# Row dot products and a softmax: the first load whole, a clearing ahead of the first y, all rows summed on VectorE, code that runs on

## The chip, the cores and the metric

The kernel runs on one core of a Trainium2 chip. The metric is the device time of one execution in microseconds (us). The kernel before takes 320.85 us, the median of three runs (320.79 to 320.87).

## The reference

The inputs x and y have the shape (8, 4096, 512) in float32. The reference forms the whole product of x and y transposed for each batch and keeps only its diagonal; what is computed is the dot product of each row of x with the same row of y, and a softmax over the 4096 dots of a batch.

```python
gram = np.matmul(x, y.transpose(0, 2, 1))
diag = np.diagonal(gram, axis1=1, axis2=2)
diag = diag - diag.max(axis=-1, keepdims=True)
exp = np.exp(diag)
return (exp / exp.sum(axis=-1, keepdims=True)).astype(np.float32)
```

## The kernel before

**Tiling.** A batch is spread over 32 partitions (G), so four batches (Q) fill the 128 partitions, and there are two groups of four. Each partition then holds 128 rows (C) of its batch. A step takes 32 rows (R) for each partition: 128 x 32 x 512 float32, which is 8.39 MB of x and as much of y. Four steps make a group, and there are eight steps (S), t = 0 to 7.

**Buffers.** There are two buffers for x (`xs`, step t uses number t % 2), one for y (`ys`) and a small one (`side`) for a copy of the last K = 6 rows of y. The dots go to `diag`, one column for each row, and `res` holds the softmax of a group.

**A step in the loop (t = 0 to 5, lines 118 to 131).** SP issues the load of x (`load_x`, line 63) and the load of y (`load_y`, line 66). ScalarE copies the last six rows of y to `side` (line 123). VectorE multiplies x by y in place: the first 26 rows from `ys`, then the last six from `side` (`products`, line 70). So `ys` can be loaded anew when the product of 26 rows and the copy are through. Then the products are summed along each row: VectorE takes the first 30 rows in one reduction (`sums`, line 73), and ScalarE the last two (W), row by row, with a copy that accumulates (`sums_act`, line 78). When both are through, the x buffer can be loaded for step t + 2.

**The first step** loads x in two parts: two rows (0.5 MB) and then thirty (7.86 MB). The y load and the x load of step 1 follow on SP without a wait.

**The order of work.** The schedule is written by hand: each engine runs its instructions in the order of the program. All loads are issued by SP and stand in one queue, in the order x(0), y(0), x(1), y(1) and so on. An issue waits for the buffer to be free, and everything behind it on SP waits with it.

**The end.** Step 6 (lines 133 to 139) loads y in two halves and multiplies each half as it lands; ScalarE sums its first 24 rows and VectorE the other eight. Step 7 (lines 141 to 150) is loaded in pieces of 16, 8, 4, 2, 1 and 1 rows, and VectorE forms the dot of each row in one instruction (`dots`, line 83). The softmax of the first group is computed between steps 3 and 4 (`exps`, `normalize`), that of the second at the end.

**Code alignment.** Lines 115 and 116 ask that the next instruction of VectorE and of ScalarE begin a block of 128 places of code. The code ahead of it then ends in a branch over the unused places.

Of the kernel before, what the change touches and what calls it, by code (L numbers as in the profile page):

```python
# [1 line left out]

# [5 lines left out]


@with_exitstack
def kernel(
    ctx: ExitStack,
    tc: tile.TileContext,
    x: bass.AP,
    y: bass.AP,
    out: bass.AP,
):
    nc = tc.nc
    ctx.enter_context(tc.manual_schedule())  # L20
    f32 = mybir.dt.float32
    Alu = mybir.AluOpType
    Act = mybir.ActivationFunctionType
    X = mybir.AxisListType.X
    B, N, D = x.shape
    P = nc.NUM_PARTITIONS
    G = 32
    Q = P // G
    C = N // G
    R = 32  # L30
    H = R // 2
    K = 6
    W = 2
    S = B // Q * (C // R)


    xv = x.rearrange("(s b) (j c) d -> s (b j) c d", b=Q, j=G)
    yv = y.rearrange("(s b) (j c) d -> s (b j) c d", b=Q, j=G)
    ov = out.rearrange("(s b) (j c) -> s (b j) c", b=Q, j=G)

    big = ctx.enter_context(tc.tile_pool(name="big", bufs=1))
    small = ctx.enter_context(tc.tile_pool(name="small", bufs=1))


    xs = [big.tile([P, R, D], f32, name=f"xs{i}") for i in range(2)]
    ys = big.tile([P, R, D], f32, name="ys")
    side = big.tile([P, K, D], f32, name="side")

    diag = [small.tile([P, C + i], f32, name=f"diag{i}") for i in range(B // Q)]
    res = [small.tile([P, C], f32, name=f"res{i}") for i in range(B // Q)]  # L50

    def columns(t, r0, n):
        c0 = t % (C // R) * R + r0
        return slice(c0, c0 + n)

    def rows(t, r0, n):
        return xs[t % 2][:, r0 : r0 + n, :]

    def dots_of(t, r0, n):
        return diag[t * R // C][:, columns(t, r0, n)]  # L60

    def load_x(t, r0, n):
        nc.sync.dma_start(out=rows(t, r0, n), in_=xv[t * R // C, :, columns(t, r0, n), :])  # L63

    def load_y(t, r0, n):
        nc.sync.dma_start(out=ys[:, r0 : r0 + n, :], in_=yv[t * R // C, :, columns(t, r0, n), :])  # L66

    def products(t, r0, n, yt):
        xt = rows(t, r0, n)
        nc.vector.tensor_tensor(out=xt, in0=xt, in1=yt, op=Alu.mult)  # L70

    def sums(t, r0, n):
        nc.vector.tensor_reduce(out=dots_of(t, r0, n), in_=rows(t, r0, n), axis=X, op=Alu.add)  # L73

    def sums_act(t, r0, n):
        for r in range(r0, r0 + n):
            row = xs[t % 2][:, r, :]
            nc.scalar.activation(out=row, in_=row, func=Act.Copy, accum_out=dots_of(t, r, 1))  # L78

    def dots(t, r0, n):  # L80
        for r in range(r0, r0 + n):
            xt = xs[t % 2][:, r, :]
            nc.vector.scalar_tensor_tensor(  # L83
                out=xt, in0=xt, scalar=1.0, in1=ys[:, r, :], op0=Alu.mult, op1=Alu.mult,
                accum_out=dots_of(t, r, 1),
            )

    def over_quadrant(name, column, op, negate=False):

        got = small.tile([P, 1], f32, name=name)  # L90
        nc.vector.tensor_reduce(  # L91
            out=got, in_=column.to_broadcast([P, G]), axis=X, op=op, negate=negate, apply_transpose=True
        )
        return got

    def largest(out, d):
        nc.vector.tensor_reduce(out=out, in_=d, axis=X, op=Alu.max)  # L97

    def exps(i, d):
        mxp = small.tile([P, 1], f32, name=f"mxp{i}")  # L100
        largest(mxp, d)
        nmx = over_quadrant(f"nmx{i}", mxp, Alu.max, negate=True)
        sump = small.tile([P, 1], f32, name=f"sump{i}")
        nc.scalar.activation(out=res[i], in_=diag[i][:, :C], func=Act.Exp, bias=nmx, scale=1.0, accum_out=sump)  # L104
        return sump

    def normalize(i, sump):
        total = over_quadrant(f"sum{i}", sump, Alu.add)
        rc = small.tile([P, 1], f32, name=f"rc{i}")
        nc.vector.reciprocal(out=rc, in_=total)  # L110
        nc.vector.tensor_single_scalar(out=res[i], in_=res[i], scalar=rc, op=Alu.mult)  # L111

    nc.vector.addr_align(128, offset=0, max_nops=0)
    nc.scalar.addr_align(128, offset=0, max_nops=0)

    for t in range(S - 2):
        if t == 0:
            load_x(t, 0, 2)  # L120
        load_x(t, 2 if t == 0 else 0, R - 2 if t == 0 else R)
        load_y(t, 0, R)
        nc.scalar.activation(out=side, in_=ys[:, R - K :, :], func=Act.Copy)  # L123
        if t == C // R:
            normalize(0, sump)
        products(t, 0, R - K, ys[:, : R - K, :])
        products(t, R - K, K, side)
        sums(t, 0, R - W)
        sums_act(t, R - W, W)
        if t == C // R - 1:  # L130
            sump = exps(0, diag[0])

    t = S - 2
    load_x(t, 0, R)
    for r0 in (0, H):
        load_y(t, r0, H)
        products(t, r0, H, ys[:, r0 : r0 + H, :])
    sums(t, R - H // 2, H // 2)
    sums_act(t, 0, R - H // 2)

    t += 1
    r0 = 0
    for n in (16, 8, 4, 2, 1, 1):
        if r0 < R - 1:
            load_x(t, r0, max(n, 2))
        load_y(t, r0, n)
        if r0 == R - 2:
            largest(diag[1][:, C:], diag[1][:, : C - 2])
        dots(t, r0, n)
        r0 += n  # L150

    met = small.tile([P, C - R], f32, name="met")
    nc.scalar.activation(out=met, in_=diag[1][:, : C - R], func=Act.Copy)  # L153

    for p, n in ((0, G), (G, G), (2 * G, G), (3 * G, G)):
        nc.sync.dma_start(out=ov[0, p : p + n, :], in_=res[0][p : p + n, :])
    normalize(1, exps(1, diag[1][:, C - 2 :]))
    nc.scalar.dma_start(out=ov[1], in_=res[1])


# [1 line left out]
_INS = ['x', 'y']  # L162
_OUTS = [((8, 4096), 'float32')]


# [23 lines left out]
```

## Time and profile before

| What | Value |
|---|---|
| median of three runs | 320.85 us (320.79 to 320.87) |
| span of the profiled execution | 318.9 us (318.87) |
| data moved | 134.37 MB, a mean of 421 GB/s |
| VectorE busy | 244.7 us, 77% of the span |
| ScalarE busy | 42.0 us, 13% |
| reduction of 30 rows (line 73) | 16.153 us each, six of them |
| reduction of 8 rows (line 73) | 4.420 us |
| product of 26 rows and of 6 rows (line 70) | 14.026 and 3.351 us |
| product of 16 rows, 128 x 8192 (line 70) | 8.684 us |
| ScalarE's sum of one row (line 78) | 0.616 us and 0.186 us to read it out |
| first issue of a load | 0.73 us after the span's start |
| first y lands | 42.33 us |

The profile shows one execution of 318.9 us; the medians of the runs hold about 2 us more than that span. Busy time is a sum over the span; which work sets the end is read from the chain of work that ended last, which is followed back from the last instruction, and from the share of time in which the 16 DMA engines carry packets. An issue on SP is the moment at which a load is handed to the queue, and a load lands when its last byte has been reported. A DMA packet here is one row of memory for one partition: up to 64 KB for a load of 32 rows.

### The profile page before, as it was taken

The page shows a single profiled execution, that of the slowest core. Times are in us where ns is not written, and L with a number is a line of the kernel's source. Part 1 is how long each engine was busy: PE and PEld are TensorE (multiplying, and loading weights), DVE is VectorE, ACT ScalarE, POOL GpSimd, SP SyncE. Part 2 cuts the span into 40 slices and gives each one's busy share as a digit, 9 for nine tenths or more (in the row PEclk, how much of TensorE's full clock was granted, in tenths as well). Part 3 has the DMA queues.
Part 4 walks back from the last instruction along what each step waited for, and adds up shares of the span by engine and source line. Part 5 has one row for each costly group of instructions (what it writes and reads, how often), then busy time and mean ns, then how long its engine had stood idle before and what let it go on. Part 6 is the DMA issues. An engine that isn't in the chain of part 4 may idle for free.

```text
span 318.9 us, 304 instructions
## 1 busy us (share of the span) xinstructions
DVE 244.7 (77%) x96; ACT 42.0 (13%) x84; POOL 0.2 (0%) x4
## 2 busy tenths in 40 slices
DVE  0000069995899939999399994999949999996995
ACT  1000030100301003010120103000030100197000
POOL 0000000000000000000000000000000000000000
DMA  8989999999999999999999999999999899999993
GB/s 314 493 378 485 436 395 436 485 395 403 510 403 395 477 444 395 427 493 395 403 510 403 395 460 460 395 419 493 403 395 510 358 444 415 444 423 419 421 413 116
DMA packets 4226, 134.37 MB, mean 421 GB/s; under 512 B 512, under 2 KB 768, under 8 KB 1536
## 3 DMA queue, kind: packets, MB, share of 16 engines
q1 hardware_dynamic: 4080, 134.29, 97.8%
q10 hardware_dynamic: 144, 0.07, 0.1%
q14 instruction: 2, 0.02, 0.0%
HBM read 134.22 MB, written 0.13 MB: 421 GB/s over the span
## 4 chain that ended last, share of the span: by engine, by line
DMA 62%; DVE 35%; issue 2%; SPq 0%; ACT 0%; DVEq 0%
DMA ys<-in_y_dram 62%; DVE xs L70 30%; DVE diag L73 4%; DVE xs L83 0%; SPq L63 0%; DVE res L111 0%; DVE nmx L91 0%; DVE sum L91 0%; ACT res L104 0%; DVE rc L110 0%; DVE mxp L97 0%; DVEq L70 0%; SPq L66 0%; DVEq L83 0%
## 5 line engine op out<-in xcount | busy, mean ns | idle before, releaser
L70 DVE TENSOR_TENSOR xs<-xs,ys 128x13312 f32<-128x13312 f32 (+1 forms) x8 | 101.4, 12690 | 66.5 <-DMA ys<-in_y_dram 66.5
L73 DVE TENSOR_REDUCE diag<-xs 128x30 f32<-128x15360 f32 (+1 forms) x7 | 101.3, 14477 | 0.2
L78 ACT ACTIVATE xs<-xs 128x512 f32<-128x512 f32 x36 | 22.2, 616 | 111.0 <-DVE xs L70 111.0
L123 ACT ACTIVATE side<-ys 128x3072 f32<-128x3072 f32 x6 | 16.6, 2764 | 124.0 <-DMA ys<-in_y_dram 124.0
L83 DVE SCALAR_TENSOR_TENSOR xs<-xs,ys 128x512 f32<-128x512 f32 x32 | 19.9, 686 | 3.3 <-DMA ys<-in_y_dram 3.3
L70 DVE TENSOR_TENSOR xs<-xs,side 128x3072 f32<-128x3072 f32 x6 | 20.1, 3351 | 0.0
L78 ACT ACTIVATION_READ_ACCUMULATOR xs<-xs 128x1 f32 x36 | 6.7, 186 | 0.0
L104 ACT ACTIVATE res<-diag,nmx 128x128 f32<-128x128 f32 x2 | 0.8, 402 | 37.6 <-DVE nmx L91 37.6
L83 DVE DVE_READ_ACCUMULATOR xs<-xs,ys 128x1 f32 x32 | 2.6, 81 | 0.0
L123 ACT ACT_TABLE_LOAD x1 | 1.3, 1283 | 1.2 <-PEq L173 1.2
L91 DVE TRANSPOSE_TENSOR_REDUCE sum<-sump 128x1 f32<-128x32 f32 x2 | 0.4, 212 | 1.2 <-ACT res L104 1.2
L111 DVE TENSOR_SCALAR res<-res,rc 128x128 f32<-128x128 f32 x2 | 0.6, 286 | 0.1
L97 DVE TENSOR_REDUCE mxp<-diag 128x1 f32<-128x128 f32 (+1 forms) x2 | 0.4, 220 | 0.1
L91 DVE TRANSPOSE_TENSOR_REDUCE nmx<-mxp 128x1 f32<-128x32 f32 x2 | 0.4, 212 | 0.1
L110 DVE RECIPROCAL rc<-sum 128x1 f32<-128x1 f32 x2 | 0.3, 164 | 0.1
L104 ACT ACTIVATION_READ_ACCUMULATOR res<-diag,nmx 128x1 f32 x2 | 0.4, 186 | 0.0
L97 DVE TENSOR_REDUCE diag<-diag 128x1 f32<-128x126 f32 x1 | 0.3, 284 | 0.1
L153 ACT ACTIVATE met<-diag 128x96 f32<-128x96 f32 x1 | 0.3, 282 | 0.0
L173 POOL MEMSET const-bfloat16-1.0<- 128x1 bf16 x1 | 0.1, 102 | 0.0
L173 POOL MEMSET const-uint8-127<- 128x1 uint8 x1 | 0.1, 102 | 0.0
L173 POOL MEMSET const-float32-0.0<- 128x1 f32 x1 | 0.1, 99 | 0.2 <-issue 0.2
L173 POOL MEMSET const-float32-1.0<- 128x1 f32 x1 | 0.1, 99 | 0.0
## 6 DMA issues: line engine op xcount, KB each, us to landing
ys<-in_y_dram SPq DMA_DIRECT2D x3, 4096.0 KB, 16.0
xs<-in_x_dram SPq DMA_DIRECT2D x1, 7680.0 KB, 21.8
xs<-in_x_dram SPq DMA_DIRECT2D x1, 4096.0 KB, 14.9
xs<-in_x_dram SPq DMA_DIRECT2D x1, 2048.0 KB, 20.5
ys<-in_y_dram SPq DMA_DIRECT2D x1, 2048.0 KB, 17.2
xs<-in_x_dram SPq DMA_DIRECT2D x3, 512.0 KB, 22.1
xs<-in_x_dram SPq DMA_DIRECT2D x1, 1024.0 KB, 19.3
ys<-in_y_dram SPq DMA_DIRECT2D x1, 1024.0 KB, 21.3
```

The costliest lines, as they stand in the source:

```text
L70: nc.vector.tensor_tensor(out=xt, in0=xt, in1=yt, op=Alu.mult)
L73: nc.vector.tensor_reduce(out=dots_of(t, r0, n), in_=rows(t, r0, n), axis=X, op=Alu.add)
L78: nc.scalar.activation(out=row, in_=row, func=Act.Copy, accum_out=dots_of(t, r, 1))
L83: nc.vector.scalar_tensor_tensor(out=xt, in0=xt, scalar=1.0, in1=ys[:, r, :], op0=Alu.mult, op1=Alu.mult, accum_out=dots_of(t, r, 1),)
L91: nc.vector.tensor_reduce(out=got, in_=column.to_broadcast([P, G]), axis=X, op=op, negate=negate, apply_transpose=True)
L97: nc.vector.tensor_reduce(out=out, in_=d, axis=X, op=Alu.max)
L104: nc.scalar.activation(out=res[i], in_=diag[i][:, :C], func=Act.Exp, bias=nmx, scale=1.0, accum_out=sump)
L110: nc.vector.reciprocal(out=rc, in_=total)
L111: nc.vector.tensor_single_scalar(out=res[i], in_=res[i], scalar=rc, op=Alu.mult)
L123: nc.scalar.activation(out=side, in_=ys[:, R - K :, :], func=Act.Copy)
L153: nc.scalar.activation(out=met, in_=diag[1][:, : C - R], func=Act.Copy)
L173: nc = _bacc.Bacc("TRN2", target_bir_lowering=False, num_devices=1)
```

## The change

The two alignment lines go. Step 0 loads its x like the other steps, in one load of 32 rows. Ahead of the y load of step 0, VectorE writes zeros to the first 16 rows of `ys`, and the load waits for that, since it writes the same rows. In steps 0 to 5 VectorE's reduction takes all 32 rows and ScalarE sums none; W is no longer needed. Step 6 keeps its sums on ScalarE.

```diff
     K = 6
-    W = 2
     S = B // Q * (C // R)
...
-    nc.vector.addr_align(128, offset=0, max_nops=0)
-    nc.scalar.addr_align(128, offset=0, max_nops=0)
-
     for t in range(S - 2):
+        load_x(t, 0, R)
         if t == 0:
-            load_x(t, 0, 2)
-        load_x(t, 2 if t == 0 else 0, R - 2 if t == 0 else R)
+            nc.vector.memset(ys[:, :H, :], 0.0)
         load_y(t, 0, R)
         nc.scalar.activation(out=side, in_=ys[:, R - K :, :], func=Act.Copy)
         if t == C // R:
             normalize(0, sump)
         products(t, 0, R - K, ys[:, : R - K, :])
         products(t, R - K, K, side)
-        sums(t, 0, R - W)
-        sums_act(t, R - W, W)
+        sums(t, 0, R)
         if t == C // R - 1:
             sump = exps(0, diag[0])
```

## The prediction

> **What bounds the kernel now.** I read the page's summary first, then the chain of work that ended last, then the DMA view in narrow windows.
>
> ```profile
> span 318.9 us, 304 instructions
> DVE 244.7 (77%) x96; ACT 42.0 (13%) x84; POOL 0.2 (0%) x4
> q1 hardware_dynamic: 4080, 134.29, 97.8%
> q14 instruction: 2, 0.02, 0.0%
> ```
>
> No engine is full, but the one data queue keeps all 16 DMA engines busy 97.8% of the span. The middle of the chain says the same:
>
> ```profile
> 1.65 40.68 DMA ys<-in_y_dram
> ...
> 81.12 14.04 DVE xs L70
> 95.16 0.02 SPq L66
> 95.18 0.03 issue
> 95.21 24.52 DMA ys<-in_y_dram
> 119.73 0.03 issue
> 119.75 0.02 DVEq L70
> 119.78 0.04 issue
> 119.82 14.04 DVE xs L70
> 133.86 0.02 SPq L66
> 133.88 0.03 issue
> 133.91 24.52 DMA ys<-in_y_dram
> ```
>
> The reader is to see where the y loads land: 42.33, 119.73 and 158.43 us. The last two are 38.70 apart, for 16.78 MB (one x and one y of 8.39 MB), which is 433.5 GB/s, or 27.1 per DMA engine. The chain seems to pass through VectorE's products, but during these 14 us the load of x that was queued earlier fills the DMA engines. So the end is the start of the first load, plus all bytes at 433.5 GB/s, plus a tail, as long as each load is issued before the one ahead of it has run out. The windows that follow show the two places where that can change; a digit is the busy share of one slot, a number under it the GB/s that began in the slot.
>
> The window 114 to 122 us, in slots of 0.2 us:
>
> ```profile
> DMA  9070000009999070000007999070000007999770
> GB/s 1638 0 328 0 0 0 0 0 0 655 983 1638 1638 0 328 0 0 0 0 0 0 328 983 1638 1966 0 328 0 0 0 0 0 0 328 983 1311 1966 328 328 0
> ```
>
> Each engine begins a packet of 64 KB every 2.4 us. The group from 118.2 to 119.4 is the first of the x load that was issued at 114.67, and it follows the group before without a gap. The window 3 to 5 us, in slots of 0.05 us:
>
> ```profile
> DMA  9939599999299938999909099000900000000000
> GB/s 410 328 164 573 246 246 246 328 328 246 82 1393 2540 1311 164 246 246 1393 1311 2458 0 4997 0 2458 1311 0 0 0 1229 0 0 0 0 0 0 0 0 0 0 0
> ```
>
> The high numbers are the 16 engines going over from the 4 KB packets of the two-row load to the 60 KB packets of the other thirty rows, the first at 3.55 us and the last at 4.40 to 4.45.
>
> **The change, part by part.**
>
> *x of step 0 in one load.* The two-row load is 8 packets of 4 KB on each engine. The first begins at 1.75 us (the window 0 to 2 us is empty before). At 27.1 GB/s an engine needs 8 x 0.151 = 1.21 us for them; the last engine is through only at 4.45, as if it had begun at full rate at 3.24. With one load, each engine goes straight into 64 KB packets. If all engines began at 1.75, the gain were 3.24 - 1.75 = 1.49 us. If their first packets were spread as widely as those long packets, 0.9 us, the gain were 0.59. The trace has no first packet of 64 KB, so these are the bounds, with a gain of nothing kept as a rival. I take the middle, **-1.0 us**. Nothing takes it back on the way: every later load stands in the same queue, and y lands when the DMA is through.
>
> *The clearing.* 128 x 8192 elements on VectorE. The nearest row is the product of that size, 8.68 us; from 0.8 us it ends at 9.5, and SP issues y of step 0 then instead of at 1.65. It is needed when the first engine is through with x, 1.75 + 19.35 = 21.1 us, less the 1.0 us from an issue (0.73) to its first packet (1.75): about 20.1. So 10.6 us are spare, and even at twice the row (17.4 us) it is hidden. Behind the waiting issue on SP stands only x of step 1, needed after y, near 41 us. VectorE has nothing to do before 42.46. Against a slower DMA beside VectorE: y of step 0 landed 19.35 us after x (22.98 to 42.33) with VectorE idle, and half of 38.70 is also 19.35. Cost 0; without the cover, 8.7.
>
> *The sums.* VectorE reduces 32 rows instead of 30 in six steps. The rows with 30 (16.153 us) and 8 (4.420 us) give 0.533 us a row, so 17.22, which is +1.07. SP's issue of x two steps on waits for this reduction (76.02, 114.67 and so on): 114.67 becomes 115.73. VectorE then works 14.03 + 3.35 + 17.22 = 34.6 us of each 38.7, so it stays ahead, and y, issued behind the products, isn't moved. The first engine asks for that x at 118.2, so the issue has 2.47 us in place of 3.53, against the 1.0 us of the first load. The later issue is hidden, **0**, by the last packet of y on each engine; without this cover it costs up to 1.07 on each of six loads. ScalarE loses 12 row sums that ended at 99.8 when VectorE's ended at 114.6; nobody waits for them: 0. The step after the loop begins its products 1.07 us later against the DMA, so the first y of the last step is issued at 279.1 instead of 278.04; the x ahead of it lands at 284.3 (269.44 + 14.9), so 5.2 us are left: 0. VectorE ends that step's reduction at 292.1, and the y lands at 294.04: 0. From there every row dot follows a landing and moves with it.
>
> Here a page speaks against the change. The Trainium skill's "DMA: Bandwidth & Descriptors" (Specifications; Latency and other measured facts) has 0.6 us to a first byte from SP, and up to 2 us for an HBM access at high load. An estimate from it is 2.6 us, 0.1 more than the issue has; six loads at 0.1 would make the sum 320.6. No row here shows a late issue under load.
>
> *No new code block.* The two branches at the start (0.72 on ScalarE, 0.76 on VectorE) go; nothing waited for them. The two instruction packets of 8 KB came at 1.75 to 3.5 us, after ScalarE had begun its table load at 1.16 behind the branch, so code is fetched ahead. Now the code runs on from the middle of a block, and the fetch of a next one may fall anywhere, or be left out. At 27.1 GB/s it takes one engine 0.30 us; both took 1.38 us of one engine's time at the start (4.3% of 16 engines for 2 us). A load lands with its slowest engine, so the cost lies between 0 and 1.38; the low end is the nearer, as one engine in sixteen is seldom the last. I take half a packet, **+0.15 us**.
>
> The page "Runtime: NRT & Kernel Launch" (Instruction fetch mechanics) calls the cost of passing into the next block mostly hidden, which would make the sum 319.85, and it has blocks of 16 KiB where the trace has packets of 8.
>
> The sum is -1.0 + 0.15 = -0.85 us on the profiled 318.87, so 318.02; the median of 320.85 lies 1.98 above that span, and I add the same: **320.0 us**.
>
> **The rivals.**
>
> - *The opening isn't shortened.* The delay to 4.45 us may come from the first accesses rather than from the packets' size, and long packets meet it too. For it: some engines take more than the others although each has 8 equal packets. Against it: a 64 KB packet holds 2.4 us of work to hide a late descriptor, a 4 KB one 0.15. Then 320.85 plus the code fetch, 320.7 to 321.1.
> - *The x loads come late*, the rival on the other side. Its place is the issue behind each of the six reductions; it decides once an issue under load takes more than 2.47 us to its first packet, and it costs six times the excess, at most 6 x 1.07 = 6.4. At 2.8 us it is +2.0, so 322.0; at the most 326.4. For it: the cover shrinks by a third. Against it: 1.0 us at the start, and no gap now.
> - *VectorE waits for code.* 66 of its 96 instructions run in the last 20 us, where it goes from dot to dot with about 0.6 us of gaps in all. A fetch that isn't ahead takes 1.0 us to its packet and half of the 1.38 for it, and behind a 64 KB packet 2.4 more: 1.7 to 4.1 us, less 0.6, so 321.1 to 323.5. Against it: the block behind the old branch was there already.
>
> **How the numbers follow.** The forecast gets 0.64, its own range being 319.3 (the whole 1.49 and no fetch) to 320.45 (0.59 and 0.2 of fetch); the opening without gain 0.14, late x loads 0.08, waiting for code 0.10, and something unseen 0.04, half to either side. Within 0.2% means within 0.64 us, about what a measurement of this kernel can tell from no change. Faster, under 320.21: 0.58 of the forecast and 0.02 unseen, 0.60. The same: 0.06 of the forecast, 0.12 of the first rival, 0.02 of the code, 0.20. Slower: 0.20. For 8 times in 10 the range takes the forecast and the first rival: 319.4 to 321.0.
>
> **What would show it.** Right: x of step 0 lands near 22.0 us, y of step 0 near 41.3, y loads still 38.70 apart, and x issues some 4 us ahead of a landing. If y loads stand further apart, the cover was too thin; if x lands near 23, the split cost nothing; if VectorE shows a gap of microseconds between dots, it waited for code. An instruction packet in the middle that shifts all later landings would mis-size my 0.15.

## The result

The changed kernel takes 321.31 us, the median of 12 runs (320.78 to 321.78), against 320.85 for the kernel before (12 runs, 320.65 to 320.99). The ratio is 1.0015, its interval 1.0008 to 1.0022: a little slower, by less than the 0.64 us that the prediction called a difference. The forecast of 320.0 was wrong, and 321.31 lies outside its range. Note the spread: 1.0 us now, 0.34 before; 9 of the 12 runs now lie above 321.0, none of the 12 before. The profiled execution belongs to a run of 320.97, so it is one of the better ones.

The summary of the page after the change:

```profile
span 319.2 us, 269 instructions
DVE 258.1 (81%) x97; ACT 33.9 (11%) x60; POOL 0.2 (0%) x4
q1 hardware_dynamic: 3936, 134.29, 97.7%
q14 instruction: 2, 0.02, 0.0%
```

VectorE has 13.4 us more work, ScalarE 8.1 less, and the data queue is as full as it was. So the bound is the same, and the difference has to be looked for where the queue starts, where it slips, and in the tail. The chain that ended last, after the change (start, duration, what):

```profile
2.50 6.90 DVE ys L117
9.40 0.02 issue
9.42 32.78 DMA ys<-in_y_dram
...
56.43 24.46 DMA ys<-in_y_dram
...
95.07 24.73 DMA ys<-in_y_dram
...
133.98 24.52 DMA ys<-in_y_dram
...
294.13 19.49 DMA ys<-in_y_dram
```

Three numbers tell the whole difference. The first y lands at 42.20 us (9.42 + 32.78), 0.13 earlier than before: that is all that the opening gained. The y of step 2 takes 24.73 us from issue to landing, where 24.52 is the rule: the x ahead of it came 0.21 late. The last stretch of the tail takes 19.49 us, where the chain before has 19.25, so 0.24 more:

```profile
294.06 19.25 DMA ys<-in_y_dram
```

Together -0.13 + 0.21 + 0.24 = +0.32, and the spans differ by 0.3. An instruction packet stands in the slow part of that tail, in the window 298 to 299 us:

```profile
q1 hardware_dynamic: 35, 0.43, 104.2%
q14 instruction: 1, 0.01, 2.0%
```

The opening, in the window 0 to 4 us (slots of 0.1 us):

```profile
DMA  0000000000000000099900990900909900000000
GB/s 0 0 0 0 0 0 0 0 0 0 0 0 0 0 0 0 0 1311 1966 1311 0 0 1966 655 0 1311 0 0 655 0 655 655 0 0 0 0 0 0 0 0
```

All 16 engines get their first 64 KB packet here, the first at 1.7 us but the last only at 3.1 to 3.2. From 3.17 a full load of 19.35 us and about 0.4 to the report of its last byte give 22.9; x of step 0 lands at 0.73 + 22.2 = 22.9, by the DMA view. The engine that starts last sets the landing, so the late starters ate the gain.

### The profile page after: what moved, and what is told of

Read it like the earlier page. It is cut to its first block, busy times and chain, and to the rows that moved or that the text cites. A ratio compares the mean times of both kernels' runs of the same rounds, so it can differ in the third digit from the quotient of the medians.

```text
span 319.2 us, 269 instructions
## 1 busy us (share of the span) xinstructions
DVE 258.1 (81%) x97; ACT 33.9 (11%) x60; POOL 0.2 (0%) x4
## 4 chain that ended last, share of the span: by engine, by line
DMA 60%; DVE 37%; issue 3%; ACT 0%; DVEq 0%; SPq 0%
DMA ys<-in_y_dram 60%; DVE xs L69 30%; DVE diag L72 4%; DVE ys L117 2%; DVE xs L82 0%; DVE res L110 0%; DVE nmx L90 0%; DVE sum L90 0%; ACT res L103 0%; DVE rc L109 0%; DVE mxp L96 0%; DVEq L69 0%; SPq L65 0%
## 5 line engine op out<-in xcount | busy, mean ns | idle before, releaser
L72 DVE TENSOR_REDUCE diag<-xs 128x32 f32<-128x16384 f32 (+1 forms) x7 | 107.7, 15391 | 0.2
L77 ACT ACTIVATE xs<-xs 128x512 f32<-128x512 f32 x24 | 14.7, 616 | 40.4 <-DVE xs L69 40.4
L117 DVE MEMSET ys<- 128x8192 f32 x1 | 6.9, 6885 | 2.5 <-issue 2.5
L77 ACT ACTIVATION_READ_ACCUMULATOR xs<-xs 128x1 f32 x24 | 4.5, 189 | 0.0
```

Of the source, the lines that this page charges most:

```text
L117: nc.vector.memset(ys[:, :H, :], 0.0)
```

## The experiments

My theory after the result: the six longer reductions make x loads late by a varying amount, and this is the loss; the opening and the code fetches nearly cancel. Rivals: the code fetches are the loss, or the clearing is. Four kernels each take the kernel before and do one part of the change alone.

**One load for x of step 0.**

```diff
-        if t == 0:
-            load_x(t, 0, 2)
-        load_x(t, 2 if t == 0 else 0, R - 2 if t == 0 else R)
+        load_x(t, 0, R)
```

> The kernel before with one edit: x of step 0 in one load. Theory now (the whole load starts its engines one after another, so nothing is gained): x of step 0 lands within 0.2 us of 22.98, time 320.6 to 320.9. The prediction's step (each engine goes straight into long packets): x lands near 22.0, time near 319.85.

320.82 us (320.72 to 320.90), ratio 1.0002 (0.9993 to 1.0010). x of step 0 lands at 23.16 us, 0.17 later than in the profile before. Four more profiles here have the opening of the kernel before, and in them it lands at 22.85 to 23.10, so neither these 0.17 nor the 0.13 above are clear of chance. Nothing is gained.

**All rows summed by VectorE.**

```diff
-        sums(t, 0, R - W)
-        sums_act(t, R - W, W)
+        sums(t, 0, R)
```

> The kernel before with one edit: VectorE sums all 32 rows in steps 0 to 5, ScalarE none. Theory now (the cover of 2.5 us is too thin for some of the 16 engines): 321.0 to 321.5 with runs further apart than the 0.2 us of before, and some x loads that take 0.1 to 0.5 us more than 19.35. Rival (the prediction's step, still covered): 320.85, all loads 19.35 apart.

321.08 us (320.74 to 321.94), ratio 1.0011 (1.0002 to 1.0020): slower, and widely spread, as this theory has it. The profiled run was one of the best (320.83), and its y loads take 24.48 to 24.60 us, so this one profile alone doesn't show late loads.

**No alignment.**

```diff
-    nc.vector.addr_align(128, offset=0, max_nops=0)
-    nc.scalar.addr_align(128, offset=0, max_nops=0)
```

> The kernel before with one edit: the two alignment lines are left out. Theory now (two code fetches move to the tail, and one hits an engine that lands last): +0.25, so 321.1, with instruction packets after 280 us. Rival (the prediction's bounds at their low end): 320.85. If the fetches at the start had cost anything, it would be under 320.8.

321.28 us (320.71 to 321.49), ratio 1.0012 (1.0003 to 1.0021). Its profile is of the fastest run and shows both sides. In the chain:

```profile
1.64 40.08 DMA ys<-in_y_dram
...
277.43 16.50 DMA ys<-in_y_dram
293.94 19.43 DMA ys<-in_y_dram
```

The first y lands at 41.72, 0.61 earlier than before: two rows ahead, with no code fetch beside them, open better than either kernel does. But one instruction packet falls between 256 and 268 us, and the second after 298. By its landings 0.50 us are lost at the half y load of step 6 and 0.17 in the tail.

**The clearing.**

```diff
         load_x(t, 2 if t == 0 else 0, R - 2 if t == 0 else R)
+        if t == 0:
+            nc.vector.memset(ys[:, :H, :], 0.0)
```

> The kernel before with one edit: VectorE clears 16 rows of y's buffer, and y of step 0 waits for it. Theory now and prediction: nothing, 320.85. Rival (the late issues of y and of x of step 1, or the clearing beside the load, cost time): 321.1 or more, with y of step 0 landing after 42.5.

320.64 us (320.50 to 321.45), ratio 0.9999 (0.9990 to 1.0007). It costs nothing that the runs tell from noise, with y issued at 9.96 us; that rival is out.

Next the change is undone part by part, and the suspected wait is made longer.

**The kernel after with the old sums.** From here on "the kernel after" is the start:

```diff
-        sums(t, 0, R)
+        sums(t, 0, R - 2)
+        sums_act(t, R - 2, 2)
```

> The kernel after with the sums of before (VectorE 30 rows, ScalarE two). Theory now: x loads are on time again, 0.2 to 0.3 us under the kernel after, 321.0 to 321.1, and the scatter is less; the code fetches stay late. Rival (the sums cost nothing): 321.3 as the kernel after.

320.81 us (320.72 to 321.27), ratio to the kernel before 1.0002 (0.9993 to 1.0011). With one part taken back, the loss is gone, more of it than the 0.2 to 0.3 us that I expected, and the spread is halved. All its y loads in the chain stand where they should:

```profile
56.37 24.47 DMA ys<-in_y_dram
...
95.02 24.52 DMA ys<-in_y_dram
...
133.72 24.51 DMA ys<-in_y_dram
...
172.42 24.52 DMA ys<-in_y_dram
...
211.12 24.52 DMA ys<-in_y_dram
```

**The kernel after with alignment.**

```diff
+    nc.vector.addr_align(128, offset=0, max_nops=0)
+    nc.scalar.addr_align(128, offset=0, max_nops=0)
     for t in range(S - 2):
```

> The kernel after with the two alignment lines back. Theory now (the six reductions of 32 rows are the loss; the code fetches cost about the same at the start as later): 321.2 to 321.4, as the kernel after, with x of step 0 landing near 23.1. Rival (the late code fetches are the loss): 320.8 to 320.9.

321.73 us (320.91 to 323.16), ratio 1.0030 (1.0017 to 1.0044). That is above the 321.2 to 321.4 that I expected. Putting the code fetches back at the start doesn't take the loss back, so their later place isn't its cause in this kernel. The profile is of the slowest run, and shows late x loads at their clearest:

```profile
95.50 24.51 DMA ys<-in_y_dram
...
134.19 25.13 DMA ys<-in_y_dram
...
173.51 24.54 DMA ys<-in_y_dram
...
212.23 25.55 DMA ys<-in_y_dram
...
281.05 15.55 DMA ys<-in_y_dram
```

The y loads of steps 3 and 5 land 0.6 and 1.0 us late, the first of step 7 0.6 (14.94 in the kernel after). These 2.2 us are most of the 2.5 by which this span (321.4) is longer than that before. The window 196 to 204 us, in slots of 0.2 us, lies around the second of them, the x issued at 193.99:

```profile
DMA  9980909080099908789007700997907977700797
GB/s 983 983 328 0 983 0 328 0 328 0 0 655 983 655 0 328 328 328 983 0 0 328 328 0 0 983 983 328 983 0 328 655 328 328 328 0 0 328 1638 328
```

Before the change each group of 16 packets lay within 1.2 us, with empty slots between the groups. Here the groups smear over nearly the whole window, and each load lands with its last engine.

**One and two more rows.** Two kernels lengthen the wait further; each starts from the kernel before, and sums rows that are summed already:

```diff
-        sums(t, 0, R - W)
-        sums_act(t, R - W, W)
+        sums(t, 0, R)
+        sums(t, R - 1, 1)
```

> The kernel before, but VectorE sums 32 rows in steps 0 to 5 and the last row once more: x is issued some 1.8 us later than before, 3.3 us ahead of a landing (4.0 in the kernel after, 2.8 with two more rows). Theory now (some engine is reached only 3 us or more after an issue): slips of 0.2 to 1 us at several loads, 321.8 to 324.5. If the knee lay below 3.3 us: 321.0 to 321.4, as with 32 rows.

The other has `sums(t, R - W, W)` as its second added line.

> The kernel before, but VectorE sums all 32 rows in steps 0 to 5 and then its last two rows once more, so x is issued some 2.3 us later than before. Theory now (an issue needs up to 2.4 us at the start and 3.2 us under load to reach its last engine, and the earliest engine is through 1.2 us ahead of the landing): every x load slips by 0.3 to 1 us, 322.5 to 327. Rival (an issue needs the 1.0 us of the first engine alone, and the scatter of the 32 rows is chance): 320.8 to 321.2.

| VectorE sums in steps 0 to 5 | x issued ahead of the landing of y | median, us |
|---|---|---|
| 30 rows (the kernel before) | 5.0 us | 320.76 to 320.85 |
| 32 rows | 4.0 | 321.08 |
| 32 rows, and one again | 3.3 | 324.59 |
| 32 rows, and two again | 2.75 | 326.49 |

The middle column is read at the first such load of each profile: the landing of y less the issue of x. The loss grows by 0.3, then by 3.5, then by 1.9 us; the 33 rows came out just above the range that I expected, the 34 rows inside it. The chain of the kernel with 34 rows:

```profile
95.30 25.41 DMA ys<-in_y_dram
...
134.88 24.55 DMA ys<-in_y_dram
...
173.55 26.48 DMA ys<-in_y_dram
```

It also shows why not every load is late: a load that slips lets the next x be issued earlier against the queue, so the lateness comes at about every second step (x issued 2.75, 3.67, 2.81, 4.74 and 2.86 us ahead of the landing of the y before).

What a late issue does to the engines can be seen with 33 rows, where x is issued at 77.82 and lands 0.37 late. The window 79.6 to 83.6 us, in slots of 0.1 us; the first pair of rows is the kernel before, the second the kernel with 33 rows:

```profile
DMA  9999999909000000000000000999999909000000
GB/s 655 1311 655 655 1966 1311 2622 655 0 655 0 0 0 0 0 0 0 0 0 0 0 0 0 0 0 1311 1311 655 1966 1311 2621 655 0 655 0 0 0 0 0 0
DMA  0999990909900000000000000900909990999909
GB/s 0 1311 655 1311 3277 1966 0 655 0 655 655 0 0 0 0 0 0 0 0 0 0 0 0 0 0 655 0 0 655 0 655 2621 1311 0 655 1311 1311 655 0 655
```

A packet of 64 KB that begins counts 655 in its slot. In both kernels the first 16 packets of the new x begin by 80.7, and the packet records show that each follows the end of y on its engine without a gap. Before, the second packets repeat the pattern 2.4 us later. With 33 rows they are scattered, because the first ones took up to 3.4 us instead of 2.42. So this load found no engine empty; its first packets were slow. With 34 rows, where the first engine is through 1.4 us after the issue, there are gaps too, 3.4 us in all over the 16 engines, beside first packets of up to 3.4 us. In the profile with 32 rows alone some first packets take up to 3.1 us, but not on the engine that lands last, and no x lands late. Why these packets are slow can't be seen here.

**Other openings.** Two kernels start from the kernel before and split x of step 0 by partitions, 16 and then 112, or eight times every eighth partition:

```diff
+            for p, n in ((0, 16), (16, P - 16)):
+                nc.sync.dma_start(out=xs[0][p : p + n, :, :], in_=xv[0, p : p + n, columns(0, 0, R), :])
...
+            for p in range(8):
+                nc.sync.dma_start(out=xs[0][p::8, :, :], in_=xv[0, p::8, columns(0, 0, R), :])
```

> The kernel before, but x of step 0 comes as two loads of all 32 rows: 16 partitions first, then the other 112. If the opening is slow because one load hands its pieces to the 16 engines one after another over 1.4 us, a load of 16 pieces starts all of them within 0.3 us, and x lands 0.5 to 1 us earlier, 319.9 to 320.4. If 16 neighbouring partitions can't be written by 16 engines at once, x lands later than 23 us, 321 or more.

> The kernel before, but x of step 0 comes as eight loads, each of every eighth partition (16 pieces of 64 KB). As in the kernel with 16 partitions first, but the first pieces lie far apart: x lands 0.5 to 1.2 us earlier, 319.7 to 320.4, if the order of the pieces is what costs the opening; 320.8 or more if it is the first accesses or the code fetches.

341.48 and 342.16 us, some 21 us slower: x of step 0 lands at 43.9 and 44.2 us. The 16 neighbouring partitions land at 13.20, their packets taking 7.7 to 9.2 us each where 2.42 is the rule, and the 112 others 30.69 us later, which is 239 GB/s. The eight loads of every eighth partition land 4.9 to 5.1 us apart, about 206 GB/s. In the window 0 to 40 us the 16 engines are busy 98 to 101% of the time in both, so it is the packets that are slow. These two say nothing for a better opening; even with 16 pieces the engines' starts were spread to about 3.15 us, which speaks against the number of pieces as the cause of the spread.

A third kernel, without the alignment lines, has 8 and 24 rows in place of 2 and 30.

> The kernel before without the alignment lines, and with x of step 0 in loads of 8 and 24 rows instead of 2 and 30. Without alignment x of step 0 landed at 22.38 with 2 rows ahead and at 22.83 in one load. If long first packets hold up the engines that start later: between the two, 22.4 to 22.8, and the time as without alignment, 321.0 to 321.5. If any split serves: 22.4.

320.81 us (320.62 to 321.47), ratio 1.0002 (0.9993 to 1.0010), x at 22.54 us. Without code fetches at the start x of step 0 lands at 22.38 with two rows ahead, 22.54 with eight, and 22.83 to 22.88 in one load. That looks like the shorter the first packets, the better, but the first two are one profile each, and the opening of the kernel before varies by 0.25 us. The time was below what I expected, since the loss that goes with leaving out the alignment didn't show in its median. The profiled run, 321.24, is one of its slow ones, and shows a slip of another kind: from y of step 3 to x of step 5 the four loads land 19.44 to 19.52 us apart instead of 19.35, 0.48 us in all, though every x is issued 5.1 us or more ahead and no first packet is long. So not every slip here is a late issue.

**One alignment line.**

```diff
     nc.vector.addr_align(128, offset=0, max_nops=0)
-    nc.scalar.addr_align(128, offset=0, max_nops=0)
```

> The kernel before with the alignment line of VectorE alone. One code fetch at the start (VectorE's), one later (ScalarE's, near 259 us), none near 298. If each fetch costs its 0.3 us only where it meets the engine that lands last: x of step 0 lands between 22.38 and 22.98, and the time is 320.4 to 320.9. If a fetch in the middle always costs: 321.1 or more.

320.81 us (320.65 to 321.31), ratio 1.0001 (0.9993 to 1.0010), x at 22.89. One fetch at the start and one near 260 us are worth as much as two at the start. No kernel here is clearly faster than the one before.

## Why the prediction was wrong

*The bound* was read rightly: the one queue's bytes at 433.5 GB/s, from its start to a tail. Every difference above is a shift of that queue.

*x of step 0 in one load* was the step with the largest error: -1.0 us forecast, a first y 0.13 us earlier measured in the profile, and nothing (320.82) when done alone. What failed is "each engine goes straight into 64 KB packets". I bounded the spread of the first packets by that of the later ones, 0.9 us, though none of the trace's rows had a first packet of 64 KB. It is 1.4 us (1.75 to 3.17). My comparison with "as if it had begun at full rate at 3.24" was right for the kernel before; the long packets begin just as late. This is the first rival, which got 0.14. Part of the old opening's time goes with the two code fetches: in the one profile without them the split load brings x 0.6 us earlier, better than the whole load. Why the engines start so far apart isn't settled; the first packet's length may have a share, by the three sizes tried, and what happens between an issue and the engines can't be seen here.

*The sums* were the cause of the loss, and my step "the later issue is hidden, 0" is the one that failed in kind. The arithmetic held: +1.07 us, 17.22 us for the reduction, x issued 4.0 us ahead of a landing. But I compared the cover of 2.47 us (2.6 to 2.9 in the packet records of the profile after) with the 1.0 us from the first issue to the *first* engine's first packet. Two things speak against the 1.0. The changed kernel's own opening shows the last engine reached only 3.17 - 0.73 = 2.44 us after the issue. And under a full queue it isn't enough that a packet begins: with 33 rows all 16 engines had theirs without a gap, the first 1.9 us after the issue, and the load was still 0.37 us late, since first packets took up to 3.4 us instead of 2.42. My sum had the last packet of y cover the issue, and no term for slow first packets. The rival "x loads come late" had its place right, behind the six reductions, but not its mechanism, a first packet that begins late; I gave it 0.08. Its cost is milder at 32 rows than its worst case and varies from run to run: 0.21 us in the profile, 2.2 in the profile with alignment, 0.5 in the medians (321.31 against 320.81 with the old sums).

*The page against the change* was the better guide. The Trainium skill's "DMA: Bandwidth & Descriptors" (Latency and other measured facts) has up to 2 us for an HBM access at high load. With its first byte from SP that made my estimate 2.6 us, just above the cover, and a time of 320.6. The first packet here began 1.0 us after the first issue, where the page has 0.6 us to a first byte. The runs side with the warning in kind: an issue beside a full queue needs more than the 1.0 us of the first engine in an idle one.

*The clearing* was right: hidden, since y was needed far later than its issue, and alone it gives 320.64. It ended at 9.4 us, forecast 9.5.

*The code fetches* were +0.15 forecast and +0.24 in the profile's tail, where one of the two packets met an engine that lands late; the other, near 289 us, cost nothing that the landings show. What I left out is that they also leave the start. Alone, no alignment gives 321.28; with one load and the clearing besides (the old sums), 320.81; with eight rows ahead, 320.81. Why the first differs is open: its fetches cost 0.50 and 0.17 us in the one profile, those with the whole load 0 and 0.26. That a tighter start leaves no engine with time to spare would explain it, but it is argued and not shown. Nor does a late issue explain the 321.28, since 30 rows are summed there. The rival "VectorE waits for code" fell: its dots in the tail follow the landings as before.

## What to carry to other kernels

Where a full queue is the bound, a load has to be issued well before the one ahead of it has landed, and the time from an issue to its first packet in an idle queue (here 1.0 us) doesn't tell how long before. Here 5.0 us ahead of the landing was always enough, 4.0 us sometimes not, and with 33 rows, 3.3 us at the first load, four of six loads were late. Take the need from a load under traffic, and look at how long its first packets last and not only for engines that run empty. A lead that is just too short shows first as scatter from run to run (9 of 12 runs above 321.0 after the change, 4 of 55 of the kernel before in all rounds), so look at many times and not at one profile. Before a microsecond of work is moved ahead of such an issue, try the same kernel with one or two microseconds more: the knee (here between 5 and 3.3 us ahead of the landing) tells how near it is.

## What the runs showed of the hardware

- Loads over part of the partitions were slower than the 433.5 GB/s over all 128, although all 16 engines took part: about 206 GB/s over every eighth, 239 over the last 112, and packets of 7.7 to 9.2 us instead of 2.42 over the first 16.
- A first load reaches the 16 engines between 1.0 and 2.4 us after its issue, with 16 pieces as with 128.
- Some first packets of an x issued about 4 us or less ahead of the landing before it took up to 3.9 us instead of 2.42, often with no empty engine before them. With x issued 5.0 us ahead they took at most 2.6, but for one of 3.0 in the kernel that split x into 16 and 112 partitions.
- The clearing's record begins at 2.50 us and lasts 6.885, though VectorE had nothing ahead of it; its end, 9.39 us, is where 8.7 us from 0.7 would put it. Whether it began late or only its record did isn't settled.
- An instruction packet of 8 KB takes one engine 0.3 us in the middle of a full queue, and moved later landings by 0 to 0.5 us.
